# Empty steps in two queues of background work, and decode sums opened by their own first products

## The chip, the cores and the metric

The kernel runs on one core of a Trainium2 chip, as one launch. The metric is the device time of that launch in microseconds (us); lower is better. A core has a matrix engine (TensorE, in the profile PE, its weight loads PEld), a vector engine (VectorE, DVE), an activation engine (ScalarE, ACT), GpSimd (POOL) and a queue engine (SyncE, SP). Each works through its own list of instructions in order, and semaphores tie the lists together.

## The reference

One step of a layer with two parallel groups of heads, for a prompt of 1024 tokens and for 8 decode sequences of one token each. All tensors are float32.

```python
hn = rmsnorm(x, g_norm)
u = hn @ w_in                                   # 1024 x 7176
xa, za, uq, uk, uv, uo, zb, ui, uf = split(u)
# group A, RG-LRU: a causal convolution of width 4, two gates, a linear scan
xc = conv_b + sum(conv_w[j] * ext[:, j:j + S] for j in range(4))
r = sigmoid(blockdiag(xc, w_r) + b_r); i = sigmoid(blockdiag(xc, w_i) + b_i)
log_a = -8 * r * softplus(-lam); a = exp(log_a)
h = scan(h -> a * h + sqrt(-expm1(2 * log_a)) * (i * xc))
# group B, mLSTM: 4 heads of 256, chunks of 128 tokens, carried C (256 x 256), n and m
P = w * (q @ k.T); num = P @ v + g * (q @ C); den = sum(P) + g * (q @ n)
C = carry_scale * C + (decay * k).T @ v         # n and m alike
merged = concat[h * silu(za), norm(sigmoid(uo) * num / den) * silu(zb)]
y = rmsnorm(x + merged @ w_out, g_final)
```

For the decode sequences the same layer runs for one token from a given state. There the mLSTM needs the product q·C of each sequence and head with its own 256 x 256 matrix C, after C has been updated.

## The kernel before

**Main products.** The input projection is cut into units of 2 x 256 columns: `v0v1 x0y0 q0k0 x1y1 q1k1 x2y2 v2v3 q2k2 x3y3 q3k3 o0o1 o2o3 z0z1 z2z3`. The first is done while the input is normalised. Each of the other 13 is done as seven products, a block scheme with seven multiplications in place of eight, and each product in two parts (`s` in `product`). Every float32 product is three fp32r products of high and low halves (`mm3`, lines 64 to 66). So a part is 12 matmuls of 512 columns, or 24 of 256 columns in the units of v and o; a unit is 14 parts. The products alternate between two sets of PSUM banks, `kv` and `o`.

**Background work.** After each part, `pop_bg` takes steps from three queues: `bg` (1 step; 2 in the first and the last of the 13 units), `rgq` (1 step) and `dcq` (1 step after every second or third part). A step is a small function that emits a handful of instructions; the step list sets the program order of the work beside the main products.

- `rgq` holds the RG-LRU work. It has 8 channel blocks (j) in two halves (b) of 512 tokens, 16 halves in all, each with seven steps (`rg_half`, line 775): `conv1`, `conv2`, `gate_a`, `gate_b`, `decay`, `scan`, `outs`. `conv2` makes the operand `xh` (line 729 casts half of it on ACT, line 730 makes the other half on DVE); `gate_a` multiplies it on PE (line 738) into the single PSUM bank `s`, and ACT reads the result twice (line 692, tiles `rg` and `ig`). `gate_b` does the same with `xl`, into the same bank. `ig` lies in the buffer of `xh`, and the scan's result `na` in that of `xl`; each buffer is there once, so `conv2` of a half cannot write `xh` before `scan` (line 765) of the half ahead has read `ig`. `conv1` also starts loads on SP (`rg_load`, `rg_gw`), `gate_a` the next load, and `outs` two stores on POOL.
- `dcq` holds the decode steps: for each of 4 heads one `first` step and 8 `token` steps (`decode_steps`). A token scales its C on ACT, adds the outer product on DVE and starts the store; after every second token, `products` multiplies the two updated matrices by their queries on PE. Its four small products of a pair go to rows 0 to 3, 32 to 35, 64 to 67 and 96 to 99 of one PSUM bank (`qp`), and the four pairs of a head add up there. Before the first pair, one product of a row of zeros (line 900) clears all 128 rows of that bank, since the copy and the product that follow read all 128.
- When `bg`, `rgq` and `dcq` are all empty, checked after each product of a unit, `m_start` puts the first chunk of the mLSTM on `bg`: `m_open1` (which takes over the memory of the RG-LRU and decode tiles and starts loads) and for each head the three steps of `m_first`. `a` makes the scores and transposes k on PE and makes the operands `kh` and `kl` (lines 1078, 1080) and `ph` and `pl`; `b` multiplies `kh` and `kl` with v (lines 64 to 66 by way of `m_kv`); `c` multiplies `ph` and `pl` with v.

**Order.** The framework puts each engine's instructions in order when the kernel is built: the program order is the priority, and an instruction that it takes not to be ready yet can be passed by later ones. So a step's place in the queues is the earliest place of its matmuls in the PE list, not always the actual one.

The queue counts give these places. Of the 16 `gate_a` steps, the one of half n stands in the order of the code 7n steps after the first, with pauses where the queue runs dry. The last `outs` comes after the first part of unit `o2o3`; the mLSTM steps start in the fifth product of that unit and end in the fourth product of `z0z1`.

After the 13 units the kernel runs the rest of the mLSTM chunks, whose matmuls are mixed with the output projection.

Of the kernel before, what the change touches and what calls it, by code (L numbers as in the profile page):

```python
# [17 lines left out]
P = 128  # L18
T = 1024
HT = 512  # L20
NB = 8
# [28 lines left out]
def hymba_kernel(  # L50
# [7 lines left out]
    V, A, G, TE = nc.vector, nc.scalar, nc.gpsimd, nc.tensor  # L58
# [46 lines left out]
    def dconst(shape, name):  # L105

        return dpool.tile(shape, F32, tag=name, name=name)
# [4 lines left out]
    ones = dconst([P, P], "ones")  # L112
    G.memset(ones, 1.0)
    maskT = const([P, P], "maskT")
# [586 lines left out]
    def rg_half(j, b):  # L701
        fp = fpr["p"]
        pc = lambda r, n=1: PT[:, j, r:r + n]
        st = {}

        n = 2 * j + b

        def conv1():
            rg_load(n, True)
            xs = st["xs"] = rst["x", n]  # L710
            rg_load(n + 1)
            if b == 0:
                rg_gw(j + 1)
                ghi = fp.tile([P, 2, P], F32R, tag="ghi", name="ghi")
                glo = fp.tile([P, 2, P], F32R, tag="glo", name="glo")
                split(ghi, glo, fpr["graw"][j % 2])
                rst["g", j] = ghi, glo
            st["xc"] = xc = fp.tile([P, HT], F32, tag="xc", name="xc")
            V.tensor_scalar(xc, xs[:, 3:3 + HT], pc(R_CW + 3), pc(R_CB), op0=ALU.mult, op1=ALU.add)
            for t in (2, 1):  # L720
                V.scalar_tensor_tensor(xc, xs[:, t:t + HT], pc(R_CW + t), xc, op0=ALU.mult, op1=ALU.add)

        def conv2():
            xs, xc = st["xs"], st["xc"]
            V.scalar_tensor_tensor(xc, xs[:, 0:HT], pc(R_CW), xc, op0=ALU.mult, op1=ALU.add)
            st["xx"] = [fp.tile([P, HT], F32R, tag=t, name=t) for t in ("xh", "xl")]
            for n, s in enumerate(LOHI):
                x = st["xx"][n]
                A.copy(x[s], xc[s])
                V.tensor_tensor(x[LOHI[1 - n]], xc[s], x[s].bitcast(F32), op=ALU.subtract)  # L730
            if b == 1:
                V.tensor_copy(OC[:, j, 1:4], xs[:, HT:HT + 3])

        def gate(n):

            pg = ps("s", [P, 512])
            for k, w in enumerate(rst["g", j]):
                TE.matmul(pg, w[:, n, :], st["xx"][n], start=k == 0, stop=k == 1)  # L738
            return pg

        def gate_a():
            rg_load(n + 1, True)
            pg = gate(0)
            st["rg"], st["ig"] = (fp.tile([P, HT], F32, tag=t, name=m) for m, t in (("rg", "rg"), ("ig", "xh")))
            gate_out(st["rg"], st["ig"], pg, j, 0)

        def gate_b():
            pg = gate(1)
            gate_out(st["rg"], st["ig"], pg, j, 1)
            st["na"] = fp.tile([P, HT], F32, tag="xl", name="na")  # L750
            A.activation(st["na"], st["rg"], AF.Tanh, scale=sp2[:, j:j + 1], bias=sp2[:, j:j + 1])
            A.activation(st["rg"], st["rg"], AF.Exp, scale=sp4n[:, j:j + 1], bias=sp4n[:, j:j + 1])
            V.scalar_tensor_tensor(st["ig"], st["ig"], 1.0, st["xc"], op0=ALU.add, op1=ALU.mult)

        def decay():
            rg, na = st["rg"], st["na"]
            V.scalar_tensor_tensor(na, rg, 1.0, na, op0=ALU.add, op1=ALU.mult)
            V.tensor_scalar(rg, na, -1.0, 1.0, op0=ALU.mult, op1=ALU.add)
            V.scalar_tensor_tensor(na, na, 2.0, na, op0=ALU.subtract, op1=ALU.mult)
            A.activation(na, na, AF.Sqrt, scale=-0.25)  # L760

        def scan():
            rg, ig, na = st["rg"], st["ig"], st["na"]
            V.tensor_tensor(ig, ig, na, op=ALU.mult)
            V.tensor_tensor_scan(na, rg, ig, 0.0 if b == 0 else OC[:, j, 0:1], op0=ALU.mult, op1=ALU.add)
            V.tensor_copy(OC[:, j, 0:1], na[:, HT - 1:HT])

        def outs():
            na, zs = st["na"], rst["z", n]
            V.scalar_tensor_tensor(na, na, 0.5, zs, op0=ALU.mult, op1=ALU.mult)  # L770
            mh, ml = sg([P, HT], "rmh", F32R), sg([P, HT], "rml", F32R)
            split(mh, ml, na)
            stq(d_rm[0, j, :, b * HT:(b + 1) * HT], mh.bitcast(F32))
            stq(d_rm[1, j, :, b * HT:(b + 1) * HT], ml.bitcast(F32))
        return [conv1, conv2, gate_a, gate_b, decay, scan, outs]

    def rg_dec(j):

# [51 lines left out]
    ds_ = {}  # L830
# [32 lines left out]
    def decode_steps(h):  # L863

        p2 = fpr["p"]
        qsel, selq = fpr["qsel"], fpr["selq"]
        st = {}

        def first():
            st["kw"] = kw = p2.tile([P, 2, NB], F32, tag="kw", name="kw")  # L870
            V.tensor_tensor(kw, dk[:, 2 * h:2 * h + 2, :], dW[:, :, h].unsqueeze(1).to_broadcast([P, 2, NB]), op=ALU.mult)
            V.tensor_copy(qsel.rearrange("p k (m r) -> p k m r", r=9)[:, :, :, 0:5:4],
                          dq[:, 2 * h:2 * h + 2, :].rearrange("p k (m r) -> p k m r", r=2))
            fetch_v(h, 0)

        def token(b):
            i = h * NB + b

            def f():
                vb_, C = ds_.pop(("v", i)), ds_["C", i]  # L880
                A.mul(C, C, dGI[:, b, h:h + 1])
                for kb in range(2):
                    V.scalar_tensor_tensor(C[:, kb, :], vb_, st["kw"][:, kb, b:b + 1], C[:, kb, :],
                                           op0=ALU.mult, op1=ALU.add)
                stq(s_C[0, b, h].rearrange("(kb p) v -> p kb v", p=P), C)
                if b + 1 < NB:
                    fetch_v(h, b + 1)
                if b % 2:
                    late.append(lambda: late.append(products))
                else:  # L890
                    fetch_C(i + 2)
                    fetch_C(i + 3)


            def products():
                if b == 1:
                    st["pq"] = ps("qp", [P, 512])
                pq = st["pq"]
                if b == 1:
                    TE.matmul(pq[:, 0:256].rearrange("p (a t) -> p a t", a=2), maskT[0:1, :],  # L900
                              ones[0:1, :].unsqueeze(1).to_broadcast([1, 2, P]), start=True, stop=False)
                for g in range(4):
                    bb, kb = b - 1 + g // 2, g % 2
                    TE.matmul(pq[32 * g:32 * g + 4, 0:256], qsel[:, kb, 4 * bb:4 * bb + 4], ds_["C", h * NB + bb][:, kb, :],  # L904
                              start=False, stop=b == NB - 1)
                for bb in (b - 1, b):
                    del ds_["C", h * NB + bb]
                if b == NB - 1:
                    Z = sg([P, 256], "qC")
                    V.tensor_copy(Z, pq[:, 0:256])  # L910

                    def turn():
                        pt = pq[:, 256:272].rearrange("p (v b) -> p v b", v=2)
                        for vb in range(2):
                            TE.matmul(pt[:, vb, :], Z[:, vb * P:(vb + 1) * P], selq, start=True, stop=True)
                        V.tensor_copy(dqC[:, 2 * h:2 * h + 2, :], pt)
                    late.append(lambda: late.append(turn))
            return f
        return [first] + [token(b) for b in range(NB)]
# [174 lines left out]
    def m_first(n):  # L1094

        def a():
            if n > 0:
                m_g(n - 1)
            if 0 < n < NH - 1:
                so_load(n + 1)  # L1100
            m_k(n)
            m_a(n)
            if n + 2 < NH:
                m_load(n + 2)

        def b():
            for kb, kv in enumerate(m_kv(n, ("qp", "s"))):
                V.tensor_copy(mx["Cf"][n][:, kb, :], kv)
        def c():
            pv = ps("qp", [P, 258])  # L1110
            mm3(pv, it[n]["ph"], it[n]["pl"], *mx["v"], True, True)
            hh = mx["p"].tile([P, 257], F32, tag="hh", name="hh", bufs=5)
            V.tensor_copy(hh, pv[:, 0:257])
            it[n]["hh"] = hh
            if n == NH - 1:
                m_g(n)
        return [a, b, c]

    def m_b(n):
        c, h = n // 4, n % 4  # L1120
# [307 lines left out]
    for n in range(4, N):  # L1428
        c, h = n // 4, n % 4
# [90 lines left out]
```

## Time and profile before

| | us |
|---|---|
| median of 3 runs | 969.24 |
| lowest and highest run | 966.21, 971.65 |
| span of the profiled execution | 973.6 |
| PE busy in it | 940.9 |
| DVE busy | 715.7 |
| ACT busy | 584.7 |
| POOL busy | 146.2 |

The profiled execution is one of its own: its span, from the first to the last instruction, is 1.95 us above the highest of the three timed runs, and no other time of it is listed. PE is busy for 97% of the span. A matmul's end in the profile is modelled and overlaps the next matmul, so the distance between two starts shows what a matmul takes of the engine; "idle before" gives only the part of a wait that is beyond the modelled end.

### The profile page before, as it was taken

To read this page: it belongs to the slowest core of one execution; us is meant where nothing else is said; L and a number is where in the kernel's file an instruction comes from. 1 tells how busy PE (TensorE), PEld (TensorE's weight loads), DVE (VectorE), ACT (ScalarE), POOL (GpSimd) and SP (SyncE) were. 2 spreads that over 40 slices of the span, in tenths; PEclk is the share of its full clock that TensorE was granted. 3 is DMA by queue.
4 is the path that set the end of the run, shared out by engine and by line. 5 is a ranking of instruction groups with operands and counts; after the bars stand their busy time and mean duration, and the time that the engine had idled before them with its cause. 6 is when DMAs were issued, how large, how long until landed. Compare 5 with 4: busy or idle time off the path is not lost.

```text
span 973.6 us, 15435 instructions
## 1 busy us (share of the span) xinstructions
PE 940.9 (97%) x5378; PEld 765.3 (79%) x5378; DVE 715.7 (74%) x1482; ACT 584.7 (60%) x1044; POOL 146.2 (15%) x258
## 2 busy tenths in 40 slices
PE   7999998999999999999999999999899999999997
PEld 7887766777787987677889897876477888888886
DVE  6776798889898878787796846576565776666764
ACT  5553436778777777654777844646445466456643
POOL 1111112112212122202221211010100100000020
PEclk9999999999999999999999999999999999999999
DMA  5431446355745555447645463425963744564471
GB/s 190 136 125 43 130 125 229 137 190 188 260 143 198 179 174 173 158 126 241 197 155 163 153 183 101 132 81 172 296 209 105 204 136 128 154 176 140 118 114 52
DMA packets 131363, 153.71 MB, mean 158 GB/s; under 512 B 15798, under 2 KB 110038, under 8 KB 131278
## 3 DMA queue, kind: packets, MB, share of 16 engines
q1 hardware_dynamic: 113558, 96.86, 34.2%
q0 software_dynamic: 17728, 55.87, 16.1%
q8 instruction: 42, 0.69, 0.4%
q14 instruction: 35, 0.29, 0.1%
HBM read 101.11 MB, written 51.65 MB: 157 GB/s over the span
## 4 chain that ended last, share of the span: by engine, by line
PE 65%; DVE 12%; DMA 10%; issue 9%; ACT 2%; POOL 1%; SPq 1%; ACTq 0%; DVEq 0%; POOLq 0%
PE ps_o L66 11%; PE ps_o L64 11%; PE ps_o L65 10%; PE ps_kv L64 7%; PE ps_kv L66 7%; PE ps_kv L65 7%; DMA W<-d_alpha 3%; PE ps_tr L227 2%; DMA raw<-in_w_in_dram 2%; DVE wl L71 2%; PE ps_tr L1206 1%; PE ps_s L738 1%; DMA oraw<-in_w_out_dram 1%; PE ps_s L1070 1%; PE ps_qp L904 1%
## 5 line engine op out<-in xcount | busy, mean ns | idle before, releaser
L70 ACT CAST wh<-raw 128x1024 fp32r<-128x1024 f32 x91 | 95.3, 1049 | 62.0 <-PE ps_o L65 22.7
L71 DVE TENSOR_TENSOR wl<-raw,wh 128x1024 fp32r<-128x1024 f32 x91 | 110.9, 1219 | 26.3 <-ACT wh L70 14.7
L64 PE MATMUL ps_kv<-cb_hi,wh 128*128 128x512 f32 x320 | 128.3, 401 | 0.2 <-ACT s L308 0.2
L66 PE MATMUL ps_kv<-cb_hi,wl 128*128 128x512 f32 x320 | 126.2, 394 | 0.0
L65 PE MATMUL ps_kv<-cb_lo,wh 128*128 128x512 f32 x320 | 125.3, 392 | 0.0
L64 PE MATMUL ps_o<-cb_hi,wh 128*128 128x512 f32 x240 | 95.6, 398 | 0.0
L66 PE MATMUL ps_o<-cb_hi,wl 128*128 128x512 f32 x240 | 94.6, 394 | 0.0
L65 PE MATMUL ps_o<-cb_lo,wh 128*128 128x512 f32 x240 | 94.0, 392 | 0.0
L64 PEld LDWEIGHTS ps_kv<-cb_hi,wh 128*128 128x128 f32 x320 | 60.4, 189 | 24.5 <-issue 5.1
L66 PEld LDWEIGHTS ps_kv<-cb_hi,wl 128*128 128x128 f32 x320 | 60.3, 189 | 15.6 <-issue 2.5
L65 PEld LDWEIGHTS ps_kv<-cb_lo,wh 128*128 128x128 f32 x320 | 60.3, 188 | 11.9
L64 PE MATMUL ps_o<-wo,rh 128*128 128x512 f32 (+1 forms) x136 | 53.9, 396 | 1.7 <-DMA rh<-d_rm 1.7
L64 PE MATMUL ps_kv<-wh,cb_hi 128*128 128x256 f32 x192 | 55.3, 288 | 0.0
L65 PE MATMUL ps_kv<-wl,cb_hi 128*128 128x256 f32 x192 | 54.3, 283 | 0.0
L66 PE MATMUL ps_kv<-wh,cb_lo 128*128 128x256 f32 x192 | 54.3, 283 | 0.0
L64 PEld LDWEIGHTS ps_o<-cb_hi,wh 128*128 128x128 f32 x240 | 45.5, 189 | 10.9 <-issue 1.7
L66 PEld LDWEIGHTS ps_o<-cb_hi,wl 128*128 128x128 f32 x240 | 45.4, 189 | 10.7 <-issue 0.8
L66 PE MATMUL ps_o<-wo,ml 128*128 128x512 f32 (+1 forms) x136 | 52.3, 385 | 0.8 <-DVE ml L71 0.7
L64 PE MATMUL ps_o<-wo,mh 128*128 128x512 f32 (+1 forms) x136 | 52.9, 389 | 0.0
L65 PEld LDWEIGHTS ps_o<-cb_lo,wh 128*128 128x128 f32 x240 | 45.5, 190 | 9.3
L66 PE MATMUL ps_o<-wo,rl 128*128 128x512 f32 (+1 forms) x136 | 52.2, 384 | 0.1
L65 PE MATMUL ps_o<-wo,rh 128*128 128x512 f32 (+1 forms) x136 | 52.1, 383 | 0.0
(470 smaller groups left out, 2546.7 us busy)
## 6 DMA issues: line engine op xcount, KB each, us to landing
raw<-in_w_in_dram SPq DMA_DIRECT2D x56, 512.0 KB
Cb<-in_state_mlstm_C_dram SPq DMA_DIRECT2D x32, 256.0 KB
out_dram<-Cb POOLq DMA_DIRECT2D x32, 256.0 KB, 4.4
qk<-d_qk SPq DMA_DIRECT2D x32, 256.0 KB
oraw<-in_w_out_dram SPq DMA_DIRECT2D x16, 512.0 KB
d_qk<-s POOLq DMA_DIRECT2D x24, 256.0 KB, 3.5
x<-in_x_prompt_dram SPq DMA_DIRECT2D x8, 512.0 KB
d_x<-s POOLq DMA_DIRECT2D x16, 256.0 KB, 3.0
```

Source lines behind the costliest of these rows:

```text
L64: TE.matmul(out, ah, bh, start=first, stop=False, skip_group_check=True)
L65: TE.matmul(out, ah, bl, start=False, stop=False, skip_group_check=True)
L66: TE.matmul(out, al, bh, start=False, stop=last, skip_group_check=True)
L70: A.copy(hi, src)
L71: V.tensor_tensor(lo, src, hi.bitcast(F32), op=ALU.subtract)
L227: TE.matmul(pz[32 * g:32 * g + 32, :], hnd[:, k, :], raws[u, k // 4][:, k % 4, :], start=k < 4, stop=k >= 4, skip_group_check=True)
L738: TE.matmul(pg, w[:, n, :], st["xx"][n], start=k == 0, stop=k == 1)
L904: TE.matmul(pq[32 * g:32 * g + 4, 0:256], qsel[:, kb, 4 * bb:4 * bb + 4], ds_["C", h * NB + bb][:, kb, :], start=False, stop=b == NB - 1)
L1070: TE.matmul(S, qk[:, 2 + kb, :], qk[:, kb, :], start=kb == 0, stop=kb == 1)
L1206: TE.matmul(dec_o[0][32 * g:32 * g + 32, :], md, oraw[m][:, half * 512:(half + 1) * 512], start=n == 0, stop=n == 14, skip_group_check=True)
```

## The change

Three edits. An empty step is put between `conv2` and `gate_a` of every RG-LRU half, so a half takes eight steps of `rgq`. An empty step is put between `a` and `b` of every `m_first`, so a head takes four steps of `bg`. The product of zeros is dropped: the first pair of a head's decode products now takes 32 columns of `qsel` in place of 4, so that the four products write all 128 rows, and each opens its sum itself. The rows beyond the first four of each group then hold products that the next step multiplies by zeros.

```diff
@@ rg_half
-        return [conv1, conv2, gate_a, gate_b, decay, scan, outs]
+        return [conv1, conv2, lambda: None, gate_a, gate_b, decay, scan, outs]
@@ decode_steps, products
                 pq = st["pq"]
-                if b == 1:
-                    TE.matmul(pq[:, 0:256].rearrange("p (a t) -> p a t", a=2), maskT[0:1, :],
-                              ones[0:1, :].unsqueeze(1).to_broadcast([1, 2, P]), start=True, stop=False)
+                n = 32 if b == 1 else 4
                 for g in range(4):
                     bb, kb = b - 1 + g // 2, g % 2
-                    TE.matmul(pq[32 * g:32 * g + 4, 0:256], qsel[:, kb, 4 * bb:4 * bb + 4], ds_["C", h * NB + bb][:, kb, :],
-                              start=False, stop=b == NB - 1)
+                    TE.matmul(pq[32 * g:32 * g + n, 0:256], qsel[:, kb, 4 * bb:4 * bb + n], ds_["C", h * NB + bb][:, kb, :],
+                              start=b == 1, stop=b == NB - 1, skip_group_check=True)
@@ m_first
-        return [a, b, c]
+        return [a, lambda: None, b, c]
```

## The prediction

> **What bounds the kernel now.** I read the head of the page first, then the groups of PE by line and shape, then PE's waits.
>
> ```profile
> span 973.6 us, 15435 instructions
> PE 940.9 (97%) x5378; PEld 765.3 (79%) x5378; DVE 715.7 (74%) x1482; ACT 584.7 (60%) x1044; POOL 146.2 (15%) x258
> PE ps_s L738 <- DVE xh L730: 4.5, 4, 2.4
> PE ps_s L738 <- ACT ig L692: 3.7, 4, 1.7
> PE ps_o L64 <- DMA rh<-d_rm: 1.7, 1, 1.7
> PE ps_qp L66 <- DVE kl L1080: 1.3, 1, 1.3
> PE ps_qp L64 <- ACT kh L1078: 0.5, 1, 0.5
> ```
>
> PE is the bound: 940.9 of 973.6 us. So a change can only win what PE waits or what it need not do. The waits (columns: total us, times, longest) that the three edits can touch are the gate products' 4.5 us on `xh` and 3.7 on `ig`, and 1.3 + 0.5 us of the first mLSTM items. That is 10 us, about 1%, and it caps the whole affair but for the product of zeros and the clock.
>
> **The product of zeros.** The timeline of PE at the first and second pair of the first head (columns: start, us, what):
>
> ```profile
> 202.99 0.69 PE L900 MATMUL ps_qp<-ones,maskT 1*128 1x256 f32 x2
> 203.62 0.61 PE L904 MATMUL ps_qp<-Cb,qsel 128*4 128x256 f32 x8
> 204.16 0.50 PE L64 MATMUL ps_kv<-cb_hi,wh 128*128 128x512 f32 x1
> ...
> 225.27 0.61 PE L904 MATMUL ps_qp<-Cb,qsel 128*4 128x256 f32 x8
> 225.81 0.66 PE L235 MATMUL ps_tr<-idF,Z 128*128 128x128 f32 x4
> ...
> L900 PE MATMUL ps_qp<-ones,maskT 1*128 1x256 f32 x8 | 2.8, 426 | 0.0
> ```
>
> With zeros a call takes 204.16 - 202.99 = 1.17 us from start to the next matmul, without 225.81 - 225.27 = 0.54. That is 0.63 us, and two records of eight make a call, so four calls: **-2.5 us**, all on PE's own path. The 32-column products are not in the trace with 256 columns of data. The nearest rows are their weight loads (min/median/max ns):
>
> ```profile
> L904 PEld LDWEIGHTS ps_qp<-Cb,qsel x128: 82/84/86, 203.6 to 565.6; 128*4 128x4 f32 x128
> L1206 PEld LDWEIGHTS ps_tr<-oraw,mAd x32: 106/108/109, 659.1 to 688.5; 128*32 128x32 f32 x32
> ```
>
> A 32-column load takes 108 - 84 = 24 ns more; eight records in each of four calls, if none is hidden, give back 0.8 us. The bounds are -1.7 and -2.5. I take -2.5, since the eight matmuls of a call start together in 0.61 us and so their loads overlap.
>
> **The gate products.** Three of the four waits on `xh`, with the matmul before each:
>
> ```profile
> 166.12 0.39 PE L64 MATMUL ps_kv<-cb_hi,wh 128*128 128x512 f32 x1
> 168.87 0.47 PE L738 MATMUL ps_s<-xh,ghi 128*128 128x512 f32 x1 [2.36 <-DVE xh L730]
> 169.18 0.40 PE L738 MATMUL ps_s<-xh,glo 128*128 128x512 f32 x1
> 169.41 0.40 PE L65 MATMUL ps_kv<-cb_lo,wh 128*128 128x512 f32 x1
> ...
> 257.59 0.39 PE L66 MATMUL ps_o<-cb_hi,wl 128*128 128x512 f32 x1
> 257.81 0.39 PE L64 MATMUL ps_o<-cb_hi,wh 128*128 128x512 f32 x1
> 258.04 0.39 PE L65 MATMUL ps_o<-cb_lo,wh 128*128 128x512 f32 x1
> 258.27 0.39 PE L66 MATMUL ps_o<-cb_hi,wl 128*128 128x512 f32 x1
> 259.52 0.47 PE L738 MATMUL ps_s<-xh,ghi 128*128 128x512 f32 x1 [0.86 <-DVE xh L730]
> ...
> 381.85 0.39 PE L64 MATMUL ps_kv<-cb_hi,wh 128*128 128x512 f32 x1
> 383.18 0.47 PE L738 MATMUL ps_s<-xh,ghi 128*128 128x512 f32 x1 [0.95 <-DVE xh L730]
> ```
>
> Main matmuls start 0.227 us apart (257.59 to 258.27 is three of them), so a part of 12 is 2.72 us: that is the slack that an empty step gives a gate product. Beyond that cadence the three lose 168.87 - 166.12 - 0.23 = 2.52, 259.52 - 258.27 - 0.23 = 1.02, and 383.18 - 381.85 - 0.23 = 1.10 us. Each is shorter than a part. Why `xh` is late, at the second of them:
>
> ```profile
> 254.72 0.62 ACT L729 CAST xh<-xc 64x512 fp32r<-64x512 f32 x1 [0.63 <-DVE na L765]
> 258.69 0.68 DVE L730 TENSOR_TENSOR xh<-xc,xh 64x512 fp32r<-64x512 f32 x1
> ```
>
> The cast waits for the scan of the half ahead, which reads `ig` in the same buffer, and the DVE half ends at 259.37. This is a ring: gate, scan, cast, gate. PE comes round it every seven parts and is now and then early; with eight parts it comes 2.72 us later and the ring itself is no longer. So 1.02 us goes.
>
> The rows at 168.87 and 383.18 are another case: the gate stands inside an `mm3` triple (L64, gate, L65), so the framework placed it by its own idea of when `xh` is ready, later than the code does. By my count of steps, the code's new place for the one at 383 is a whole unit later (each half adds a part, and this is the eleventh): there code order decides, and 1.10 goes. For the one at 168.87, the second half, the new place is the end of the part before the one that it already stands in; the empty step need not move it, and its 2.52 us may stay. I take **-2.1 us** for the gates, with ends 0 and -4.5, the whole row of waits. The waits on `ig` (3.7) lie between `gate_a` and `gate_b`, where nothing is inserted; I leave them as they are.
>
> **The first mLSTM items.** The wait is at the third head, in `b`:
>
> ```profile
> 604.60 0.39 PE L66 MATMUL ps_o<-cb_hi,wl 128*128 128x512 f32 x1
> 605.46 0.39 PE L64 MATMUL ps_qp<-vh,kh 128*128 128x258 f32 x1 [0.48 <-ACT kh L1078]
> 605.69 0.28 PE L65 MATMUL ps_qp<-vl,kh 128*128 128x258 f32 x1
> 607.27 0.38 PE L66 MATMUL ps_qp<-vh,kl 128*128 128x258 f32 x1 [1.30 <-DVE kl L1080]
> 607.49 0.28 PE L64 MATMUL ps_s<-vh,kh 128*128 128x258 f32 x1
> 607.61 0.28 PE L65 MATMUL ps_s<-vl,kh 128*128 128x258 f32 x1
> ...
> 604.00:608.36 4.36, 2.58 (x14) 1.77 (x13) 4.36 (x10) 1.96 (x4) 0.00 (x0) 1.00 0.15 38
> 608.40:611.77 3.37, 3.37 (x10) 2.63 (x9) 1.39 (x4) 0.65 (x2) 0.58 (x1) 0.50 0.25 91
> 130.50:133.90 3.40, 3.31 (x12) 3.05 (x13) 3.22 (x7) 0.67 (x6) 0.82 (x3) 0.50 0.23 82
> ```
>
> Start to start it costs 605.46 - 604.60 - 0.23 = 0.63 and 607.27 - 605.69 - 0.12 = 1.46 (0.12 is the step from 607.49 to 607.61): **-2.1 us**. One part of 2.72 covers it, by 0.6 us. The windows show what follows: from 608.4 to 611.8 the granted clock (third number from the end) is 0.50. Half of 3.4 us is lost, **-1.7 us** more, if the wait is what brings it on. The only other such row inside the main products, 130.5 to 133.9, also follows a wait of about 2 us, so I take it so.
>
> [...]
>
> **What moves.** Each half takes one part more. The last `outs` goes, by the step count, from the first part of `o2o3` to its sixth, `m_start` by one product (two parts), and the last `m_first` step from the fourth to the seventh product of `z0z1`. All are in place before `z2z3`, whose steps keep their places. The loads that `conv1`, `gate_a` and `m_open1` start on SP move with their users; the last stores of `outs` on POOL come five parts later, and their reader is the `rh` load whose wait stands above, for the output projection after the last unit. Two whole units, 28 parts, still lie between, so I count that as nothing; without that cover the 1.7 us wait on `rh` would grow. No wait is added.
>
> **Sum**: -2.5 - 2.1 - 2.1 - 1.7 = -8.4 us on a span of 973.6. The median of the runs is 4.4 us lower than that span; I take the difference over as it is: 969.2 - 8.4 = **960.8 us**, -0.87%.
>
> **Rivals.** About 0.5%, or 4.8 us, is what a measurement of this kernel can tell from no change.
>
> - The second half's gate moves as well, and the ring's slack also takes the short waits: another 2.5 us, **958.3**. For it: the wait is under one part. Against: its place inside a triple.
> - The clock is not won: another wait fills a window, such as the 2.52 us at 166, which this time fell across two. -6.7 us, **962.5**. [...]
> - The wait changes its name: `gate_a` runs later, `gate_b` is still one part behind it, ACT gets to the gate's result no sooner, and what is won on `xh` comes back on `ig`; a new wait of 2 us keeps the clock loss. -2.5 - 2.1 = -4.6, **964.6**, on the edge. For it: `ig` already costs 3.7.
> - The empty steps do nothing, since the framework orders by readiness and each matmul stays where it was: -2.5, **966.7**. Against: the gate at 259.52 stands at a part's end, as the code puts it.
> - Slower: ACT becomes the late engine. The halves now fall on other places of the units, and every one of the 16 second gate products waits on `ig` as long as the longest now, 1.7 us: 27.2 - 3.7 = +23.5, less 8.4, is +15.1, **984**. It decides from about ten such waits (10 x 1.7 = 17, that is 13.3 more than now, and 4.9 beyond the 8.4). Against: ACT is busy 60% of the span, and only four waits are in the row.
>
> **How the numbers follow.** Forecast 0.35, clock not won 0.15, both gates 0.12, wait renamed 0.20, empty steps idle 0.12, slower 0.06. The first three are faster by over 0.5%, together 0.62, with a little of the fourth 0.63. The rest of the fourth and the fifth are 0.30, and slower gets 0.07. The range runs from 956.0, 2.3 us under the best case for scatter of the runs, to 967.5, 0.8 us over the case of -2.5, where the 0.8 us of the weight loads is in. Only the slower case lies outside, and tails of the others.
>
> **What would show it.** L900 gone, and a first-pair call of 0.54 us. No idle before L738 from `xh` but for the one near 168. No idle on `kl`, and a clock of 1.00 around 608. The forecast is wrong if `ig` or another wait of PE has grown by what `xh` lost, or if PE's span falls by less than its waits do.

## The result, and the profile after

The changed kernel takes 960.09 us in the median of 4 runs (958.95 to 962.38), against 969.12 us before (the three runs of the table above and a fourth): 0.9904 of the time, with a 95% interval of 0.9878 to 0.993. The forecast was 960.8 us, so the total came out as forecast. Its terms did not, as the experiments show. One execution of a later combination (the change with its step between the gates and without the mLSTM step) took 1843.33 us and is left out of its ratio.

The span of the profiled execution fell further than the median, from 973.6 to 958.2 us. The head of the page and PE's waits after the change (waited for: total us, times, longest), as far as they answer to those shown of before or are new:

```profile
span 958.2 us, 15403 instructions
PE 930.4 (97%) x5370; PEld 760.4 (79%) x5370; DVE 714.4 (75%) x1482; ACT 583.9 (61%) x1044; POOL 146.3 (15%) x258
...
PE ps_qp L64 <- ACT hh L1124: 3.0, 1, 3.0
PE ps_o L64 <- DMA rh<-d_rm: 1.7, 2, 1.4
PE ps_s L822 <- DVE ORow L823: 1.3, 1, 1.3
PE ps_s L738 <- ACT ig L692: 1.1, 3, 0.8
PE ps_s L738 <- DVE xh L730: 1.0, 1, 1.0
PE ps_tr L1204 <- DMA oraw<-in_w_out_dram: 0.4, 2, 0.2
```

The waits of the gate products are down from 4.5 + 3.7 to 1.0 + 1.1 us, so 6.1 us are gone where the forecast had 2.1. The waits on `kh` and `kl` have left the list. All rows of the list add up to 25.4 us before and 20.0 after, so some 2.5 us of the 7.9 that left these rows have come back in others. Two larger ones are new: 1.3 us on `ORow` and 3.0 us on `hh`. For the second, the timeline of ACT in the changed kernel (start, us, what, idle before):

```profile
692.77 1.15 ACT L1213 ACTIVATE wo<-oraw,gm 128x1024 fp32r<-128x1024 f32 x1 [1.28 <-DMA oraw<-in_w_out_dram]
698.98 1.15 ACT L1213 ACTIVATE wo<-oraw,gm 128x1024 fp32r<-128x1024 f32 x1 [5.06 <-DMA oraw<-in_w_out_dram]
700.03 0.39 ACT L70 CAST qh<-qk 128x256 fp32r<-128x256 f32 x1
700.33 0.62 ACT L70 CAST Ch<-Cf 128x516 fp32r<-128x516 f32 x1
700.85 0.47 ACT L1124 ACTIVATE hh<-ps_qp,gi_t 128x257 f32<-128x257 f32 x1
```

ACT stands behind a transfer of the output weights until 698.98, and what PE waits for is queued behind that. Before the change PE met the same late transfer under another name, the 2.1 us on `oraw` itself (now 0.4):

```profile
PE ps_tr L1206 <- DMA oraw<-in_w_out_dram: 2.1, 2, 1.9
```

So PE waits 3.0 + 0.4 - 2.1 = 1.3 us more here than before. The row on `hh` is no mark of the empty steps: it is there, with 3.2 us, when only the zeros are dropped.

The first call of the decode products without the product of zeros (start, us, what), and all weight loads of that line (min/median/max ns):

```profile
198.59 0.64 PE L902 MATMUL ps_qp<-Cb,qsel 128*32 128x256 f32 x8
199.15 0.50 PE L64 MATMUL ps_kv<-cb_hi,wh 128*128 128x512 f32 x1
...
L902 PEld LDWEIGHTS ps_qp<-Cb,qsel x128: 82/85/109, 198.6 to 551.9; 128*4 128x4 f32 x96, 128*32 128x32 f32 x32
```

From start to the next matmul it takes 0.56 us in place of 1.17: 0.6 us in each of four calls, 2.4 us. The wider loads cost 20 ns or so of a call, and not the 0.2 us of the bound.

Last the clock. In the profile of before it is 0.50 in five windows of 3.41 us, which begin at 11.0, 31.5, 130.5, 608.4 and 703.9 us, and once more at the very end. In the profile of after it is 1.00 from 6.9 to 955.8 us. A stretch of after (granted clock third from the end), and then the mean clock of the two executions:

```profile
40.00:940.00 900.00, 884.97 (x5049) 720.04 (x5048) 679.68 (x1398) 556.92 (x985) 140.61 (x240) 1.00 0.52 163
...
core 0: 973.6 us, clock 0.989
...
core 0: 958.2 us, clock 0.999
```

That difference is worth up to 10 us of the 15.4 us between the spans ((1 - 0.989) x 973.6 against (1 - 0.999) x 958.2), and most of it is luck: of the five windows only the one at 608.4 was forecast to go. In the 73 runs of the kernel before that the experiments gave, the clock has a mean of 0.9935 and the time follows it (correlation -0.78): runs at 0.999 took 966.1 and 966.9 us, those at 0.988 took 974.0 and 979.2 us. The profile of before was one of the worst of its kind, and that of after has the highest clock of the 17 runs of its own. This goes most of the way to explain why the medians differ by 9 us and the spans by 15.

### The profile page after: what moved, and what is told of

It reads as the page before. It is cut to its first block, busy times and chain, and to the rows that moved or that the text cites. A ratio compares the mean times of both kernels' runs of the same rounds, so it can differ in the third digit from the quotient of the medians.

```text
span 958.2 us, 15403 instructions
## 1 busy us (share of the span) xinstructions
PE 930.4 (97%) x5370; PEld 760.4 (79%) x5370; DVE 714.4 (75%) x1482; ACT 583.9 (61%) x1044; POOL 146.3 (15%) x258
## 4 chain that ended last, share of the span: by engine, by line
PE 70%; DVE 11%; DMA 10%; ACT 4%; issue 4%; SPq 1%; POOL 0%; ACTq 0%; DVEq 0%; POOLq 0%
PE ps_o L66 12%; PE ps_o L64 12%; PE ps_o L65 12%; PE ps_kv L64 7%; PE ps_kv L66 7%; PE ps_kv L65 7%; DMA Cb<-in_state_mlstm_C_dram 2%; PE ps_tr L227 2%; DMA W<-d_alpha 2%; PE ps_s L738 1%; PE ps_s L1068 1%; DVE wl L71 1%; DMA raw<-in_w_in_dram 1%; PE ps_tr L1204 1%; DMA oraw<-in_w_out_dram 1%
```

## The experiments

The main theory was the one on record: PE is the bound, and each edit takes away its own work or waits. The rival was that any edit re-deals the order in which the framework lists the instructions. All ratios are to the kernel before on the same chip.

**One edit at a time: the zeros.**

```diff
-                if b == 1:
-                    TE.matmul(pq[:, 0:256].rearrange("p (a t) -> p a t", a=2), maskT[0:1, :],
-                              ones[0:1, :].unsqueeze(1).to_broadcast([1, 2, P]), start=True, stop=False)
+                n = 32 if b == 1 else 4
...
-                              start=False, stop=b == NB - 1)
+                              start=b == 1, stop=b == NB - 1, skip_group_check=True)
```

> Only the product of zeros is dropped; no empty step. Main theory (PE is the bound, so its own work counts in full): four first-pair calls fall from 1.17 to 0.57 us as in the changed kernel's trace, -2.4 us, and all other waits of PE stay. Rival (the order of the engines is re-dealt by any edit, and the gain is luck of the order): waits on xh and ig change too, by more than 1 us, and the time moves by something else than 2.4.

Measured: 1.0015 (0.9993 to 1.0036), so no gain at all, and -2.4 us (0.9975) lies outside. PE's waits in its profile, those that grew:

```profile
PE ps_s L738 <- DVE xh L730: 4.9, 5, 2.1
PE ps_s L738 <- ACT ig L692: 4.5, 4, 2.3
PE ps_qp L64 <- ACT hh L1124: 3.2, 1, 3.2
PE ps_s L1174 <- DVE ms L1144: 1.4, 3, 0.6
PE ps_qp L64 <- ACT kh L1076: 1.4, 1, 1.4
PE ps_o L66 <- DVE ml L71: 1.4, 1, 1.4
```

All waits of PE in the list add up to 25.4 us before and to 30.3 us here. PE has 2.4 us less to do and waits 4.9 us more in this execution, part of it for the output weights as above. The rows on `xh` and `ig` moved by 0.4 and 0.8 us, so neither theory has it whole. That the saved work was not time because the other engines did not come earlier as well is the reading that fits. It rests on one profile, though, and that is of the slowest of the 12 runs (976.33 us, with a median of 971.46). What re-deals the waits in detail was not followed up.

**The gates' empty step alone.**

```diff
-        return [conv1, conv2, gate_a, gate_b, decay, scan, outs]
+        return [conv1, conv2, lambda: None, gate_a, gate_b, decay, scan, outs]
```

> Only the empty step ahead of gate_a. Main theory (a ring of gate, scan, cast and gate round which PE comes one part later): PE's wait on xh falls from 4.5 to about 1, the wait on ig from 3.7 to about 1, as in the changed kernel's trace, in all -6 us; the 1.8 us at the first mLSTM items stays. Forecast on record: -2.1 us. Rival (the whole gain is the clock and the zeros): under -2 us.

Measured: 0.9948 (0.9929 to 0.9967), some 5 us. The main theory holds for the waits:

```profile
PE ps_s L738 <- DVE xh L730: 1.3, 2, 0.8
PE ps_s L738 <- ACT ig L692: 1.3, 3, 0.8
```

And a thing that neither had said: no row on `kh` or `kl` is left, though the mLSTM items have no empty step here. By the count of steps the longer halves delay their start by two parts, and the third head no longer meets the late operand.

**The mLSTM items' empty step alone.**

```diff
-        return [a, b, c]
+        return [a, lambda: None, b, c]
```

> Only the empty step in the first mLSTM items. Main theory: the 1.8 us of waits on kh and kl go, and the half-speed window behind them with it, -2.1 us start to start and up to -1.7 more; waits on xh and ig stay at 4.5 and 3.7. Rival (the clock window falls by chance and the next stage waits for a transfer anyway): the waits go, the time moves by under 1 us, as the output projection then waits longer for w_out.

Measured: 0.9974 (0.9951 to 0.9997), 2.5 us with an interval that almost reaches no change. The waits on `kh` and `kl` are gone and those on `xh` and `ig` are where they were (4.4 and 3.5), as the main theory had it. The mean clock of its 12 runs is 0.9936, that of the 35 runs of the kernel before on that chip 0.9933: the half-speed window is not saved by this step in the mean of the runs. Its own profile, without those waits, has a mean clock of 0.997.

**The buffer that was to make `xh` late.** The input of the scan goes into the spent buffer of `xs`, so that `ig`, in the buffer of `xh`, is free as soon as it has been read once.

```diff
-            V.scalar_tensor_tensor(st["ig"], st["ig"], 1.0, st["xc"], op0=ALU.add, op1=ALU.mult)
+            st["u"] = st["xs"][:, 0:HT]
+            V.scalar_tensor_tensor(st["u"], st["ig"], 1.0, st["xc"], op0=ALU.add, op1=ALU.mult)
...
-            rg, ig, na = st["rg"], st["ig"], st["na"]
+            rg, ig, na = st["rg"], st["u"], st["na"]
```

> No empty step, zeros kept; the input of the scan is written into the spent buffer of xs and not back into the one that xh shares, so the cast of xh need not wait for the scan of the half ahead. Main theory (the ring through that buffer makes xh late): the wait on xh falls from 4.5 to under 1.5 us with seven steps as before, and ACT's wait on the scan (11.9 us in 7 times) is gone; -3 us. Rival (what counts is only that PE comes later, since DVE and ACT are behind with all their work): the wait on xh stays over 3 us.

Measured: 1.0022 (1.0002 to 1.0042). ACT's waits ahead of the cast, first before and then here:

```profile
ACT xh L729 <- DVE na L765: 11.9, 7, 3.9
ACT xh L729 <- DVE xc L725: 4.4, 3, 2.4
```

```profile
ACT xh L729 <- DVE xc L725: 7.7, 7, 2.6
...
PE ps_s L738 <- DVE xh L730: 2.7, 2, 1.4
PE ps_s L738 <- ACT ig L692: 3.9, 5, 2.5
```

The tie to the scan is cut: the row with 11.9 us is gone. In its place the cast waits for the convolution that feeds it, PE still waits 2.7 us on `xh` and as much as ever on `ig`, and the time is not better. Half by half it is less simple. At the sixth half, the one at which the prediction read the ring, `xh` is now ready at 254.40, 5.1 us ahead of its matmul, with seven parts as before; the 2.7 us are at the first half, which has no half ahead of it, and at the seventh:

```profile
253.71 0.69 DVE L730 TENSOR_TENSOR xh<-xc,xh 64x512 fp32r<-64x512 f32 x1
...
259.53 0.39 PE L738 MATMUL ps_s<-xh,ghi 128*128 128x512 f32 x1
...
147.54 0.47 PE L738 MATMUL ps_s<-xh,ghi 128*128 128x512 f32 x1 [1.36 <-DVE xh L730]
...
287.04 0.47 PE L738 MATMUL ps_s<-xh,ghi 128*128 128x512 f32 x1 [1.38 <-DVE xh L730]
```

Neither theory has the 2.7 us. The buffer's tie did make `xh` late where the prediction said so, but cutting it only moves the waits to other halves. The edit also holds each of the two buffers of `xs` until the scan, so the last load into them starts at 504.0 us, not at 478.4; DVE's wait for these loads at the head of the convolution is 3.5 us, against 2.8 before.

**Both empty steps, and the whole change again on the same chip.** The first has the product of zeros, the second is the change itself.

> Both empty steps, the product of zeros kept. The product of zeros dropped alone gave 1.0015 of the time before, not 0.9975. Theory A (PE's saved 2.4 us count only where its other waits do not grow, and with the empty steps they do not): this kernel is 2 to 3 us slower than the whole change, about 0.993. Theory B (dropping the zeros is worth nothing, and the whole gain is the empty steps'): it equals the whole change, about 0.9905.

> The whole change once more, on the same chip as the others of this call, to be set against them. Both theories: 0.9904 of the time before, with its interval 0.988 to 0.993. If it comes out above 0.994, the first measurement was a lucky one and the sum of the parts (0.9915 from the three single edits) is nearer.

Measured: 0.9945 (0.9926 to 0.9964) and 0.9908 (0.9891 to 0.9925). Two things follow. The mLSTM step adds nothing that can be seen to the gates' step (0.9945 against 0.9948). And dropping the zeros, which brought nothing alone, brings 3.6 us by the ratios and 2.1 us by the medians (965.93 and 963.81) in this company; the two intervals just miss each other, so its size is rough, but theory A is nearer. One row shows where more than the 2.4 us may come from. PE's wait for the copy that frees the `kv` banks, with both steps and then with the whole change:

```profile
PE ps_kv L64 <- ACT s L308: 2.5, 2, 2.0
```

```profile
PE ps_kv L64 <- ACT s L308: 0.6, 1, 0.6
```

The row goes with the zeros beside a gates' step: it has 1.1 to 2.7 us in all four kernels with both, and 0.8 us or less in all others but the one with the buffer's tie cut (0.9).

**The empty step at other places of the half.** First after `outs`, then between the two gates.

```diff
-        return [conv1, conv2, gate_a, gate_b, decay, scan, outs]
+        return [conv1, conv2, gate_a, gate_b, decay, scan, outs, lambda: None]
```

```diff
-        return [conv1, conv2, gate_a, gate_b, decay, scan, outs]
+        return [conv1, conv2, gate_a, lambda: None, gate_b, decay, scan, outs]
```

> The empty step stands after outs, at the end of each half, and not ahead of gate_a; nothing else is changed. Main theory (what counts is that a half comes round every eight parts, since its chain of gates, decay, scan and next cast takes longer than the code allows for): the wait on xh falls as with the step ahead of gate_a, to 1 to 2 us, and the time by 4 to 6 us, 0.995. Rival (what counts is the distance between conv2 and gate_a): the wait on xh stays over 3.5 us and the time within 2 us of before.

> The empty step stands between gate_a and gate_b. The half takes eight parts too, but gate_b and all behind it come one part later, so the chain from gate_b to the next gate_a has no more room than before. Main theory: the wait on ig goes (3.7 to under 0.5 us), the wait on xh stays at 3 to 5 us, the time falls by 3 to 4 us, 0.9965. Rival (fewer background steps per part help whatever stands where, since DVE and ACT get more time for everything): xh and ig both fall to 1 us or so, as with the step ahead of gate_a, 0.995.

Measured: 0.9967 (0.9953 to 0.9981) at the end, 0.9919 (0.9901 to 0.9937) between the gates. The gate products' waits, at the end and then between:

```profile
PE ps_s L738 <- DVE xh L730: 2.4, 3, 1.4
PE ps_s L738 <- ACT ig L692: 0.5, 2, 0.3
```

```profile
PE ps_s L738 <- DVE xh L730: 2.2, 3, 1.5
PE ps_s L738 <- ACT xl L729: 0.9, 1, 0.9
```

For these two waits the place of the step decides little: at every place `xh` falls from 4.5 to between 1 and 2.4 us and `ig` from 3.7 to 1.3 or less. For the time it does matter: on the same chip the step between the gates is some 4 us faster than the step at the end (medians 964.46 and 968.58), and the intervals lie apart. Why is open; all waits of PE add up to 20.2 and 20.3 us in the two profiles. With the step at the end 0.9 + 0.2 us of waits on `kh` and `kl` are left as well. In the first run the rival fails, which tied the wait to the distance of `conv2` and `gate_a`, and the main theory, nearer, asked for a little more than came. In the second the main theory fails, which said that a step between the gates leaves `xh` alone; it forecast too little, and its rival is nearer. What the three places have in common is that a half comes round every eight parts, not seven, so DVE and ACT have 14% more time for each. The timeline of the changed kernel at the sixth half, the one whose gate stood at 259.52 before:

```profile
262.23 0.62 ACT L729 CAST xh<-xc 64x512 fp32r<-64x512 f32 x1 [1.33 <-DVE na L765]
...
263.41 0.69 DVE L730 TENSOR_TENSOR xh<-xc,xh 64x512 fp32r<-64x512 f32 x1
...
272.61 0.39 PE L738 MATMUL ps_s<-xh,ghi 128*128 128x512 f32 x1
```

`xh` is ready at 264.10, 8.5 us ahead of its matmul, where it had been 0.9 us late. One part is 2.7 us, so the distance alone does not give this. The cast still follows the scan, but the DVE half then comes at once: from the start of the cast to the end of `xh` it takes 1.9 us, and before it took 4.65 (254.72 to 259.37), with other work of DVE in between. That is this one half: over all 16 the median from cast to end of `xh` is 2.3 us before and 2.4 after. What grew is the room, the time from the end of `xh` to its gate. Its median over the 16 halves, and the number of halves that have under 0.2 us of it:

| | room, us | halves without |
|---|---|---|
| before, seven parts | 0.7 | 5 |
| seven parts, buffer's tie cut | 1.9 | 5 |
| changed kernel, eight parts | 5.4 | 2 |
| eight parts, step at the end | 4.0 | 3 |
| eight parts, step between the gates | 1.7 | 5 |

In the changed kernel only the first two halves are without room; from there the engines stay ahead of PE, and the 1.0 us that is left on `xh` is the wait of the first half. The step between the gates gives little room here, as the chain from `gate_b` to the next `gate_a` gets no more time, and yet it has the best time of the three places. So the room at `xh` explains the waits on `xh`, not the whole gain.

**Combinations.** The whole change with its step between the gates; the same without the mLSTM step; the whole change with both gate steps, nine parts for a half; and the whole change once more. The first three, each against the changed kernel:

```diff
-        return [conv1, conv2, lambda: None, gate_a, gate_b, decay, scan, outs]
+        return [conv1, conv2, gate_a, lambda: None, gate_b, decay, scan, outs]
```

```diff
-        return [conv1, conv2, lambda: None, gate_a, gate_b, decay, scan, outs]
-        return [a, lambda: None, b, c]
+        return [conv1, conv2, gate_a, lambda: None, gate_b, decay, scan, outs]
+        return [a, b, c]
```

```diff
-        return [conv1, conv2, lambda: None, gate_a, gate_b, decay, scan, outs]
+        return [conv1, conv2, lambda: None, gate_a, lambda: None, gate_b, decay, scan, outs]
```

> The whole change with the gates' empty step between gate_a and gate_b in place of ahead of gate_a. Alone that place gave 0.9919 and the place of the change 0.9948, and dropping the zeros was worth 0.0037 in company. Theory A (these add): 0.988, faster than the whole change of the same call by 2 to 3 us, wait on ig gone, on xh about 2 us. Theory B (once half the stalls are gone, the order decides and nothing adds): 0.991, as the whole change.

> As e9 without the empty step in the first mLSTM items. Theory A (that step is worth something only while the items stand where the next unit's preparation is made; with halves of eight parts they start later and the wait on kh and kl is gone without it, as the run with the gate step alone shows): the same time as e9 within 1.5 us, no wait on kh and kl over 0.3 us. Theory B (the step has its own worth, as the -2.5 us of the run with it alone): 2 to 3 us slower than e9, with the 1.8 us of waits back.

> The whole change and a second empty step, between gate_a and gate_b, so a half takes nine parts. Theory A (what is left on xh and ig, 2 us, is all that it can win, and the steps end later): xh and ig both under 1 us; RG-LRU work ends a unit later, so m_start is pushed back and the first mLSTM items run into the last unit, where decode outputs and w_out are prepared; 0.990 to 0.996. Theory B (fewer background steps per part go on helping): 0.986.

> The whole change a third time, to be set against the three others on the same chip: 0.9906, between 0.989 and 0.9925 by both theories.

| | ratio to before | 95% interval | PE's waits, us |
|---|---|---|---|
| whole, step between the gates | 0.9905 | 0.9872 to 0.9939 | 20.1 |
| the same without the mLSTM step | 0.9935 | 0.9908 to 0.9961 | 21.6 |
| whole, nine parts | 0.9911 | 0.9879 to 0.9942 | 20.6 |
| whole, third time | 0.9918 | 0.9888 to 0.9948 | 20.6 |

None is clearly faster than the change. For the step between the gates theory B holds: nothing adds any more. For nine parts it is theory A. In the run with nine parts `xh` and `ig` are down to 0.9 and 0.2 us, yet other waits have come up and the sum in the last column is the same as for eight. The run without the mLSTM step has no wait on `kh` or `kl`, as its theory A said, but is 3.5 us slower than the first row in the median, which is nearer to its theory B; the intervals overlap, so whether the step has a worth of its own in this company stays open. For the wait on the output weights, first the list of the first row, then of nine parts:

```profile
PE ps_qp L64 <- ACT hh L1124: 4.1, 1, 4.1
```

```profile
PE ps_tr L1204 <- DMA oraw<-in_w_out_dram: 2.8, 4, 1.0
```

It is among the largest in each, under one name or the other.

## Why the prediction was right, and where it was not

- **PE is the bound, and the waits cap the gain.** Right: PE is busy for 97% of the span in both, and the ratio of three measurements of the whole change, 0.9904, 0.9908 and 0.9918, is 8 to 9 us (by the medians 9.0, 7.9 and 6.6).
- **The product of zeros, -2.5 us, "all on PE's own path".** The size of the work was right (2.4 us less in the trace), and also the choice between the bounds. The step that failed is to count it in full whatever else is done: alone it gave 1.0015, with other waits longer in its profile; only beside the gates' step did it show.
- **The gate products, -2.1 us.** Mis-sized: 6.1 us of waits left the profile, and the step alone is worth 5 us. Two of its steps failed. The second half's 2.52 us "may stay", since the matmul's place was set by readiness. In the changed kernel PE meets it without idle time, behind a whole triple:

```profile
163.93 0.39 PE L66 MATMUL ps_kv<-cb_hi,wl 128*128 128x512 f32 x1
164.16 0.47 PE L738 MATMUL ps_s<-xh,ghi 128*128 128x512 f32 x1
```

By a count of the main matmuls it stands five later than before, 1.1 us; so the operand also came some 1.4 us earlier against them. And the waits on `ig` were left as they are, as nothing is inserted between the gates; they fell by 2.6 us. The other two waits on `xh` went as forecast. The gate of the eleventh half stands 125 main matmuls later, which is ten parts and not the whole unit of 14 that the prediction counts; its operand is now some 9 us early.
- **Why `xh` is late: the ring through the shared buffer.** Right for the sixth half, where cutting the buffer's tie makes `xh` 5.1 us early, but not what sets the waits as a whole: with the tie cut and seven parts kept, `xh` still waits 2.7 us, at other halves, and the time is no better. What the three places of the empty step have in common is the longer round of a half, and the room above fits that for two of them: DVE and ACT are just in time at many halves of seven parts, and ahead at most halves of eight. It was not tested by itself, say by taking work from DVE, and the 4 us between two of the places stay unexplained.
- **The first mLSTM items, -2.1 us.** The wait goes, as forecast, and the step alone gives 2.5 us. But in the whole change it need not be this step that removes it: the gates' step alone does, by moving the items. The step that failed is to add the two terms; as far as the wait goes they are one. Whether the mLSTM step is worth something of its own beside the others stays open (nothing to be seen beside the gates' step, some 3 us beside the step between the gates and without the zeros).
- **The half-speed window, -1.7 us.** The tie to the wait fits the two profiles. Before, 1.8 us of waits on `kh` and `kl` are followed at once by half speed, from 608.4 to 611.8 us; after, both waits are gone and the clock is 1.00 from 500 to 700 us. The step that failed is "No wait is added": half speed can follow another wait, as the prediction's own rival had it. In the second profile of the whole change it follows the wait for the output weights, 3.0 us on `hh`, and the clock is 0.50 from 701.66 to 705.07 us; in the first the same wait is there and the clock stays at 1.00. So no steady gain in clock shows: on the chip of the second measurement the mean clock is 0.9946 for the change and 0.9924 before, on that of the third 0.9948 for both. The last section has the rows.
- **What moves is free.** Right for the RG-LRU work and its stores: the wait on `rh` is 1.7 us as before. The 1.3 us on `ORow`, in the last RG-LRU step, and the 1.3 us more at the output weights were not foreseen.

So the total is right in part by luck: terms too large (the zeros and the mLSTM items, which do not count in full, and the clock) and one too small (the gates) offset each other. The prediction's sign of being wrong, another wait that grows by what `xh` lost, came in part: `xh` lost 3.5 us, and the rows on `ORow` and for the output weights together gained 2.6.

## What to carry to other kernels

Where background steps are handed out at a fixed rate beside a bound engine, look how much room their results have at the point where that engine needs them. If there is none at many places, as here at seven parts for a half, slow the whole round down first, and look for the single tie (a buffer, a place in the list) after that. Test edits in company as well as alone: here a saving on the bound engine was worth nothing by itself, and two edits that each removed the same wait did not add up. When one profile of each kernel differs by more than the medians do, look at the granted clock of both (here 0.989 and 0.999) before explaining the rest.

## What the runs showed of the hardware

In the profile of before the granted clock changes eleven times, and these changes lie whole multiples of 3.413 us apart; five stretches at half speed last 3.41 us each. After, it is 1.00 from 6.9 to 955.8 us, 278 times 3.413 us. The rows below are stretches of this length, laid end to end from the changes in each profile.

The same wait comes with and without the penalty. The wait of 2.1 us on `stk` is in the profiles of before and of after. Before, 1.97 us of idle time fall into one stretch, and the next is at half speed; after, the wait is split, 1.65 us fall into one, and the next is at full speed (stretch, length, PE busy; granted clock third from the end; two lines of before, then two of after):

```profile
127.09:130.50 3.41, 1.44 (x8) 0.87 (x6) 3.33 (x7) 0.67 (x2) 0.00 (x0) 1.00 0.20 77
130.50:133.91 3.41, 3.32 (x12) 3.06 (x13) 3.23 (x7) 0.67 (x6) 0.82 (x3) 0.50 0.23 82
...
126.39:129.80 3.41, 1.76 (x12) 1.65 (x13) 3.37 (x6) 0.27 (x1) 0.76 (x3) 1.00 0.03 5
129.80:133.21 3.41, 3.41 (x18) 2.48 (x17) 3.32 (x10) 2.10 (x8) 0.76 (x2) 1.00 0.39 118
```

So it is with the wait of 3.0 us on `hh`, which the first and the second profile of the whole change share. In the first it falls across two stretches, with 1.45 and 1.54 us idle, and the clock stays at 1.00; in the second it falls into one, with 3.02, and the next is at 0.50:

```profile
696.42:699.83 3.41, 1.96 (x14) 1.50 (x12) 0.00 (x0) 0.85 (x1) 0.00 (x0) 1.00 0.91 350
699.83:703.24 3.41, 1.87 (x12) 1.62 (x12) 3.08 (x6) 2.82 (x6) 0.00 (x0) 1.00 0.80 223
...
698.24:701.66 3.42, 0.40 (x3) 0.05 (x1) 1.26 (x2) 2.44 (x5) 0.00 (x0) 1.00 0.73 229
701.66:705.07 3.41, 3.41 (x13) 3.13 (x14) 2.82 (x9) 1.34 (x2) 0.00 (x0) 0.50 0.87 228
```

The wait of 2.52 us on `xh` at 166 us, which the prediction's rival names, is such a case before: it falls across two stretches, with 1.54 and 0.82 us idle, and the clock is 1.00 in both and in the next.

Counted over the profiles of before and after, from 40 to 945 us, there are 525 such stretches at full speed. Half speed follows the three with the most idle time, 1.76, 1.97 and 2.02 us, all of them before, and none of the other 522. At 28.1 us before, half speed also follows a stretch with 1.26 us idle; why is open. No run sets the idle time itself, so these are the waits that occurred, and no bound can be read from them.
